# Query and key halves split on 128 partitions with their copies made by DMA, and the last gate job's S5 rows loaded whole

## The chip, the cores and the metric

The kernel runs on one core of a Trainium2 chip. The metric is the device time of one execution in microseconds; the time before is the median of three runs, 1220.09 us (1220.04 to 1220.55). The core's engines are named as in the profile: PE (TensorE, matmuls), PEld (its weight loads), DVE (VectorE), ACT (ScalarE), POOL (GpSimd) and SP (SyncE), whose queue issues nearly all DMAs.

## The reference

Two layers (`DEPTH = 2`) of a block on 1024 positions of width 1024, then a last RMS norm, all in float32. Of each layer:

```python
h = rms_norm(x, norm_w[l])
proj = h @ w_in[l]
fq, fk, fv, flog, su, rq, rk, rv, gate = split_cols(proj)
logf = log_sigmoid(flog + fox_b_f[l])
y_fox = forgetting_attention(fq, fk, fv, logf)      # 8 heads of 64, causal, softmax with decay
y_s5  = s5_layer(su, ...)                           # 16 groups of a complex scan, GLU
y_ret = retention(rotary(rq), rotary(rk), rv, ...)  # 4 heads of 64, group norm
y = concatenate([y_fox, y_s5, y_ret]) * silu(gate)
x = x + y @ w_out[l]
```

The scores of the attention are `q @ k / 8 + c_query - c_key`, with c the running sum of logf, masked to the past.

## The kernel before, in words

**Precision by halves.** A matmul on float32 takes longer than one on the rounded type `float32r`. So a large operand is split into a high part (a cast to float32r) and a low part (what the cast left over), and a product is the sum of three: high x high, high x low, low x high. `XH` and `XL` hold the normed input (later the gated output) in this form; `split_w` (line 306) does it for weights, in rings of two places each: `wr` raw, `wh` high, `wl` low.

**Projections.** A "job" (line 360) is 128 columns of the input projection. `granules` (line 320) runs the jobs one after another. A job has two parts of 512 positions (four of 256 for the last gate job), and a part is 24 matmuls into one of two PSUM banks (`ps_proj`), after which the job's `ev` reads the bank out. The next job's weights are loaded and split while the current one runs.

**Attention.** The 8 heads go in 4 pairs p. Each pair has four jobs, in this order: v, g (the gate), q, k. Here is what the change touches, in `fox_jobs` (line 458). The scores of one head are two matmuls with 128 rows each: `M` holds the head's 64 query rows, high and low one above the other, `T` holds the key's high rows twice, and `KL` the key's low rows of both heads:

- head A: `MA` = query high on partitions 0 to 63, low on 64 to 127; `TA` = key high on both halves;
- head B: `MB` and `TB` the other way about; `KL` = low of A over low of B.

So the query's `ev` (lines 465 to 470) makes two casts on ACT and two subtractions on DVE on 64 partitions each, and the key's `ev` (lines 475 to 482) two casts on ACT, two subtractions and two copies of the high rows to the other half on DVE. In `fox_rows` (line 518) POOL makes `zq` (M with the low half set to zero), PE multiplies `M` with `T` and `zq` with `KL` into `ps_s`, DVE adds the decay and takes the row minimum (`P`, `mn`), ACT the exponential, DVE the scaling. `turn` (line 566) has PE transpose P into `ps_t`, splits it into `pth` (ACT) and `ptl` (DVE), and PE multiplies these with the values into `ps_o`. The jobs of pair p+1 run among the attention of pair p; those after them need the attention of p done (`free`, line 509).

**Rings.** `slot(tag, ...)` takes a place of a ring in SBUF; a tile waits until the one before it in its place has been read for the last time. `th` has 2 places (used by v, g, the gate jobs and the output projection), `pt` has 5 (also for `pth`, `ptl`, `yt`), `wl` 2.

**Gate jobs.** `gate_job(l, x)` (line 1088) gates S5 rows (x = 0, 1) and retention rows (x = 2, 3): it loads the rows `y_d[4 + x]` to `yg`, multiplies, and splits the result. Jobs 0 and 1 are the last of a layer. Job 1 writes into XH and XL directly, in four parts of 256, while `y_loads` (line 1141) brings the other six blocks of rows, 768 KB for each DMA, over the parts of XH and XL that job 1 has finished with. Then `out_first` begins.

**What sets the order.** PE's order is written by hand through a planner (`Weave`, line 32): generators yield what they need, and the one that can run soonest by the planner's own costs (lines 109 to 147) goes next. For a DMA it charges

```python
if eng == "D":
    start += 1.0
    dur = max(out.nbytes(), 16384) / 360e3
...
end = start + dur + (2.0 if eng == "D" else 0.0)
```

one after another on one queue. The planner knows the PSUM banks, not the SBUF rings. The other engines' instructions and the DMAs are put in order by the framework's scheduler, from dependences, ring places and its own estimate; every engine, SP too, then works through its list in that order. Since engine calls go through the planner's recorder, every operation has line 158 in the profile; they are told apart by tile.

Of the kernel before, what the change touches and what calls it, by code (L numbers as in the profile page):

```python
# [9 lines left out]
F32 = mybir.dt.float32  # L10
F32R = mybir.dt.float32r
I32 = mybir.dt.int32
AF = mybir.ActivationFunctionType
ALU = mybir.AluOpType
AX = mybir.AxisListType

L = 1024
# [147 lines left out]
def need(*tiles, ps=(), ev=()):  # L165
    return tiles, ps, ev
# [3 lines left out]
def hybrid_block(ctx: ExitStack, tc: tile.TileContext, a: dict, out: bass.AP, taps=None):  # L170
# [5 lines left out]
    V, S, G, PE = (Clocked(W, k, e) for k, e in (("V", nc.vector), ("S", nc.scalar), ("G", nc.gpsimd), ("P", nc.tensor)))  # L176
    dma = Clocked(W, "D", nc.sync).dma_start
# [12 lines left out]
    def nm(s):  # L190
        uid[0] += 1
        return f"{s}_{uid[0]}"

    def slot(tag, shape, dt=F32, name=None):
        return sp.tile(shape, dt, tag=tag, name=nm(name or tag), bufs=NB[tag])

    def psum(tag, shape=(128, 512)):
        t = pp.tile(list(shape), F32, tag=tag, name=nm("ps_" + tag), bufs=PSUM[tag])
        W.psum(tag, t)
        return t  # L200
# [4 lines left out]
    def fr(ap):  # L205
        return ap.bitcast(F32)
# [44 lines left out]
    for c in (slice(0, 512), slice(512, 1024)):  # L251
        ps = psum("proj")
# [12 lines left out]
    y_d = dr.tile([KB, 128, L], F32, name="y_d")  # L265
# [94 lines left out]
    def job(l, col, start, perm=False, before=(), after=(), tags=("wh", "wl"), parts=2):  # L360
        src = a["w_in"][l, :, col:col + 128].rearrange("(k p) c -> p k c", p=128)
        return (lambda: split_w(src, 128, perm, tags)), start, before, after, parts

    def silu2(g2):

        def ev(n, sl, ps):
            th = slot("th", [128, 512], F32, "th")
            S.activation(out=th, in_=ps, func=AF.Tanh, scale=0.5)
            V.scalar_tensor_tensor(out=g2[:, sl], in0=th, scalar=1.0, in1=ps, op0=ALU.add, op1=ALU.mult)
        return ev  # L370
# [86 lines left out]

    def fox_jobs(l, p, tiles):
        qt = "qb" if p % 2 else "qa"

        def start_q():
            tiles.update((n, slot(qt, [128, L], F32R, n)) for n in ("MA", "MB", "TA", "TB", "KL"))
            MA, MB = tiles["MA"], tiles["MB"]

            def ev(n, sl, ps):
                S.copy(out=MA[0:64, sl], in_=ps[0:64])
                S.copy(out=MB[64:128, sl], in_=ps[64:128])
                V.tensor_tensor(out=MA[64:128, sl], in0=ps[0:64], in1=fr(MA[0:64, sl]), op=ALU.subtract)
                V.tensor_tensor(out=MB[0:64, sl], in0=ps[64:128], in1=fr(MB[64:128, sl]), op=ALU.subtract)
            return ev  # L470

        def start_k():
            TA, TB, KL = (tiles[n] for n in ("TA", "TB", "KL"))

            def ev(n, sl, ps):
                S.copy(out=TA[0:64, sl], in_=ps[0:64])
                S.copy(out=TB[64:128, sl], in_=ps[64:128])
                V.tensor_tensor(out=KL[0:64, sl], in0=ps[0:64], in1=fr(TA[0:64, sl]), op=ALU.subtract)
                V.tensor_tensor(out=KL[64:128, sl], in0=ps[64:128], in1=fr(TB[64:128, sl]), op=ALU.subtract)
                V.tensor_copy(out=TA[64:128, sl], in_=fr(TA[0:64, sl]))  # L480
                V.tensor_copy(out=TB[0:64, sl], in_=fr(TB[64:128, sl]))
            return ev

        def start_v():
            tiles.update((n, slot("v", [128, NT, 128], F32R, n)) for n in ("VA", "VB"))

            def ev(n, sl, ps):
                vt = slot("th", [128, 512], F32, "vt")
                S.copy(out=vt, in_=ps)
                W.add(values(n, vt), 2, SLACK["val"])  # L490
            return ev

        def values(n, vt):
            yield need(vt, ps=("t",))
            pt = psum("t", (128, 4, 128))
            for b in range(4):
                PE.transpose(pt[:, b, :], vt[:, b * 128:(b + 1) * 128], ident)
            for j, vx in enumerate((tiles["VA"], tiles["VB"])):
                src = pt[:, :, j * 64:(j + 1) * 64]
                hi = vx[:, 4 * n:4 * n + 4, 0:64]  # L500
                S.copy(out=hi, in_=src)
                V.tensor_tensor(out=vx[:, 4 * n:4 * n + 4, 64:128], in0=src, in1=fr(hi), op=ALU.subtract)
            W.done.add(("v", l, p, n))

        def start_g():
            tiles["g2"] = slot("gy", [128, L], F32, "g2")
            return silu2(tiles["g2"])

        free = {0: (("ret", l),), 1: (("ret", l), ("s5", l))}.get(p, (("att", l, p - 2),))
        return [job(l, C_V + p * 128, start_v, before={0: (), 1: (("mix", l),)}.get(p, free)),  # L510
                job(l, C_G + p * 128, start_g, before=() if p == 0 else free),
                job(l, C_Q + p * 128, start_q, before=free if p else (("mix", l),)),
                job(l, C_K + p * 128, start_k, after=(("k", l, p),))]
# [574 lines left out]
    def gate_job(l, x):  # L1088

        def start():  # L1090
            if x == 1:
                W.add(y_loads(l), 4)

            def ev(n, sl, ps):
                m = ps.shape[-1]
                y = slot("pt", [128, m], F32, "yg")
                dma(out=y, in_=y_d[4 + x, :, sl])
                th = slot("th", [128, m], F32, "th")
                S.activation(out=th, in_=ps, func=AF.Tanh, scale=0.5)
                V.scalar_tensor_tensor(out=th, in0=th, scalar=1.0, in1=ps, op0=ALU.add, op1=ALU.mult)  # L1100
                V.scalar_tensor_tensor(out=y, in0=y, scalar=0.125 if x < 2 else 0.5, in1=th, op0=ALU.mult, op1=ALU.mult)
                k = XPOS[4 + x]
                if x == 1:
                    S.copy(out=XH[:, k, sl], in_=y)
                    V.tensor_tensor(out=XL[:, k, sl], in0=y, in1=fr(XH[:, k, sl]), op=ALU.subtract)
                    W.mark(f"y5{l}.{n}")
                else:
                    yh, yl = th.bitcast(F32R), y.bitcast(F32R)
                    S.copy(out=yh, in_=y)
                    V.tensor_tensor(out=yl, in0=y, in1=th, op=ALU.subtract)  # L1110
                    dma(out=ys_d[k, :, 0, sl], in_=fr(yh))
                    dma(out=ys_d[k, :, 1, sl], in_=y)
            return ev

        return job(l, C_G + (4 + x) * 128, start, perm=x < 2, before=(("s5" if x < 2 else "ret", l),), after=(("gate", l, x),),
                   parts=4 if x == 1 else 2)
# [24 lines left out]
    def y_loads(l):  # L1141

        for n in range(4):
            yield need(ev=(("att", l, 2), ("gate", l, 1, n)))
            sl = slice(n * 256, (n + 1) * 256)
            for i, x in enumerate((XH, XL)):
                dma(out=fr(x[:, 0:6, sl]), in_=ys_d[:, :, i, sl].rearrange("k p c -> p k c"))
                W.mark(f"y{l}.{n}.{i}")
            W.done.add(("y", l, n))
# [68 lines left out]
    def trunk():  # L1218
# [10 lines left out]
        for l in range(depth):  # L1229
# [9 lines left out]
            for p in range(4):  # L1239
                tiles = {}  # L1240
                js = fox_jobs(l, p, tiles)

                def start_k(start=js[3][1], p=p, tiles=tiles):
                    W.add(fox_attend(l, p, tiles), 3)
                    return start()

                jobs += js[:3] + [(js[3][0], start_k, *js[3][2:])]
# [65 lines left out]
```

## Time and profile before

| | |
|---|---|
| median of three runs | 1220.09 us |
| the profiled execution | 1219.19 us, its span 1217.5 us |
| PE | 1163.4 us busy, 96% |
| DVE | 918.2 us, 75% |
| ACT | 559.1 us, 46% |
| POOL | 210.3 us, 17% |
| DMA | 140.64 MB, 37% of 16 engines on SP's queue |
| granted clock of PE | 0.98 of 2.4 GHz in the mean |

"Span" is the time from the first to the last instruction; the execution is 1.7 us longer. PE's busy time is modelled, since matmuls are pipelined: the end of one overlaps the next. In timelines, a bracket `[idle <-releaser]` says how long the engine stood idle ahead of a row and what ended that.

### The profile page before, as it was taken

Reading aid. Unit: us, or ns where it says so; the run is one execution under the profiler, and the core shown is the slowest. Engines: PE = TensorE matmul, PEld = TensorE weight load, DVE = VectorE, ACT = ScalarE, POOL = GpSimd, SP = SyncE. Lnnn points to the kernel's source line nnn. Section 1 sums busy time; section 2 is a strip of 40 time slices with the busy share of each in tenths; the row PEclk is TensorE's granted clock in tenths of the full one; section 3 lists DMA queues with packets and bytes.
Section 4 is the critical chain, followed back from the end, with each engine's and each line's share of the span. In section 5 each row is a group of like instructions: output and inputs, shape, how many; then the busy total and the mean of one; then the engine's idle time right before and its main releaser. Section 6 shows DMA issues by size and latency. Waiting matters only on the chain.

```text
span 1217.5 us, 18685 instructions
## 1 busy us (share of the span) xinstructions
PE 1163.4 (96%) x6320; PEld 989.2 (81%) x6320; DVE 918.2 (75%) x2611; ACT 559.1 (46%) x1085; POOL 210.3 (17%) x451
## 2 busy tenths in 40 slices
PE   8999989999799899999999999999999999989997
PEld 7878867878688787878889878778888888788886
DVE  7789696478778678786877856967877868968736
ACT  6526233445455455553243364335545545645411
POOL 0016222021122121210000163211212112112000
PEclk9999988999899999999999999999999999999999
DMA  7255324431112112838341845222233121274534
GB/s 231 58 158 176 115 71 132 140 125 52 61 35 71 53 43 78 271 115 231 101 153 59 258 112 146 63 92 73 61 109 109 57 57 53 82 233 154 170 107 156
DMA packets 137538, 140.64 MB, mean 116 GB/s; under 512 B 18849, under 2 KB 108641, under 8 KB 137442
## 3 DMA queue, kind: packets, MB, share of 16 engines
q1 hardware_dynamic: 137440, 139.44, 37.0%
q8 instruction: 50, 0.82, 0.3%
q14 instruction: 46, 0.38, 0.1%
q10 hardware_dynamic: 2, 0.00, 0.0%
HBM read 99.13 MB, written 40.29 MB: 115 GB/s over the span
## 4 chain that ended last, share of the span: by engine, by line
PE 50%; DVE 10%; issue 3%; ACT 2%; DMA 2%; POOL 0%; SPq 0%; DVEq 0%; ACTq 0%; POOLq 0%
PE ps_proj L158 37%; PE ps_s L158 5%; PE ps_o L158 4%; PE ps_t L158 4%; DVE P L158 2%; DMA yg<-y_d 1%; DVE ptl L158 1%; DVE wl L158 1%; DVE s5z L158 1%; DVE x L158 1%; DMA wor<-in_w_out_dram 0%; DVE g L158 0%; DVE KL L158 0%; DVE s5b L158 0%; ACT wh L158 0%
## 5 line engine op out<-in xcount | busy, mean ns | idle before, releaser
L158 PE MATMUL ps_proj<-XH,wh 128*128 128x512 f32 (+1 forms) x864 | 229.4, 395 | 3.9 <-DVE MB L158 2.6
L158 PE MATMUL ps_proj<-XH,wl 128*128 128x512 f32 (+1 forms) x864 | 228.3, 392 | 0.0
L158 PE MATMUL ps_proj<-XL,wh 128*128 128x512 f32 (+1 forms) x864 | 225.6, 388 | 0.0
L158 PEld LDWEIGHTS ps_proj<-XH,wh 128*128 128x128 f32 x864 | 159.1, 193 | 34.9 <-issue 3.0
L158 PEld LDWEIGHTS ps_proj<-XH,wl 128*128 128x128 f32 x864 | 157.8, 191 | 30.5 <-issue 0.5
L158 PEld LDWEIGHTS ps_proj<-XL,wh 128*128 128x128 f32 x864 | 157.0, 189 | 29.9 <-issue 0.5
L158 PE MATMUL ps_proj<-wo,XH 128*128 128x512 f32 x512 | 162.7, 394 | 0.0
L158 ACT ACTIVATE P<-P,mn 128x256 f32<-128x256 f32 (+7 forms) x128 | 99.5, 777 | 85.2 <-DVE mn L158 83.4
L158 DVE TENSOR_TENSOR ptl<-ps_t,pth 128x512 fp32r<-128x512 f32 (+1 forms) x160 | 99.2, 632 | 33.0 <-ACT pth L158 31.8
L158 ACT CAST pth<-ps_t 128x512 fp32r<-128x512 f32 (+1 forms) x160 | 85.0, 542 | 67.0 <-PE ps_t L158 52.3
L158 PEld LDWEIGHTS ps_proj<-wo,XH 128*128 128x128 f32 x512 | 95.3, 188 | 18.7
L158 DVE CUSTOM_DVE_ANT_0 P<-ps_s,negc,mn 128x128 f32<-128x128 f32 (+3 forms) x176 | 97.3, 553 | 7.3 <-PE ps_t L158 0.5
L158 PE MATMUL ps_proj<-wo,XL 128*128 128x512 f32 x256 | 100.5, 393 | 0.0
L158 DVE TENSOR_TENSOR wl<-wr,wh 128x1024 fp32r<-128x1024 f32 (+1 forms) x56 | 75.4, 1348 | 29.6 <-ACT wh L158 11.8
L158 PE MATMUL ps_t<-ident,P 128*128 128x128 f32 x576 | 87.0, 278 | 2.6 <-DVE P L158 2.5
L158 ACT CAST wh<-wr 128x1024 fp32r<-128x1024 f32 (+1 forms) x56 | 66.3, 1188 | 43.7 <-PE ps_proj L158 38.0
L158 PEld LDWEIGHTS ps_t<-ident,P 128*128 128x128 f32 x576 | 69.5, 144 | 8.8 <-issue 2.2
L158 POOL TENSOR_SCALAR_AFFINE_SELECT md<-negc 128x128 f32<-128x128 f32 x128 | 49.1, 384 | 149.4 <-DVE mn L158 72.1
L158 DVE TENSOR_SCALAR P<-P,rd 128x256 f32<-128x256 f32 (+7 forms) x128 | 66.8, 523 | 2.0
L158 POOL TENSOR_TENSOR rot<-rot,c_cos 128x512 f32<-128x512 f32 x16 | 27.4, 1711 | 232.7 <-ACT rot L158 231.6
L158 PE MATMUL ps_s<-KL,zq 128*128 128x256 f32 (+1 forms) x192 | 65.8, 343 | 0.0
L158 PE MATMUL ps_o<-ptl,VA 128*128 128x256 f32 x160 | 46.0, 310 | 16.3 <-DVE ptl L158 16.2
(259 smaller groups left out, 2033.0 us busy)
## 6 DMA issues: line engine op xcount, KB each, us to landing
wr<-in_w_in_dram SPq DMA_DIRECT2D x56, 512.0 KB, 4.1
negc<-negc_d SPq DMA_DIRECT2D x16, 512.0 KB, 3.7
wor<-in_w_out_dram SPq DMA_DIRECT2D x32, 256.0 KB, 3.4
ys_d<-yt SPq DMA_DIRECT2D x24, 256.0 KB, 2.4
XL<-ys_d SPq DMA_DIRECT2D x8, 768.0 KB, 10.0
XH<-ys_d SPq DMA_DIRECT2D x8, 768.0 KB, 7.0
xt<-x_d SPq DMA_DIRECT2D x24, 256.0 KB, 3.3
x_d<-xh SPq DMA_DIRECT2D x16, 256.0 KB, 3.5
```

Source lines behind the costliest of these rows:

```text
L158: r = f(*args, **kw)
```

## The change

In `fox_jobs`, the query's and the key's bank are cast and subtracted whole, on 128 partitions, into places of the ring `th`, and DMAs of 64 partitions by 512 columns bring the halves to their rows: four for a query part (two of the high half, two of the low half), four for a key part (each high half to both halves of its T). `KL` is written by the subtraction directly. In the last gate job (x = 1) the four loads of `yg` are replaced by two loads of half a row block each, into a place of the ring `wl`, asked for in the job's `start`, ahead of `y_loads`. The other gate jobs are as before.

```diff
 def start_q():
     def ev(n, sl, ps):
-        S.copy(out=MA[0:64, sl], in_=ps[0:64])
-        S.copy(out=MB[64:128, sl], in_=ps[64:128])
-        V.tensor_tensor(out=MA[64:128, sl], in0=ps[0:64], in1=fr(MA[0:64, sl]), op=ALU.subtract)
-        V.tensor_tensor(out=MB[0:64, sl], in0=ps[64:128], in1=fr(MB[64:128, sl]), op=ALU.subtract)
+        qh, ql = (slot("th", [128, 512], F32R, x) for x in ("qh", "ql"))
+        S.copy(out=qh, in_=ps)
+        V.tensor_tensor(out=ql, in0=ps, in1=fr(qh), op=ALU.subtract)
+        for M, r in ((MA, lo), (MB, up)):
+            dma(out=fr(M[r, sl]), in_=fr(qh[r]))
+        for M, r, o in ((MA, lo, up), (MB, up, lo)):
+            dma(out=fr(M[o, sl]), in_=fr(ql[r]))
 def start_k():
     def ev(n, sl, ps):
-        S.copy(out=TA[0:64, sl], in_=ps[0:64])
-        S.copy(out=TB[64:128, sl], in_=ps[64:128])
-        V.tensor_tensor(out=KL[0:64, sl], in0=ps[0:64], in1=fr(TA[0:64, sl]), op=ALU.subtract)
-        V.tensor_tensor(out=KL[64:128, sl], in0=ps[64:128], in1=fr(TB[64:128, sl]), op=ALU.subtract)
-        V.tensor_copy(out=TA[64:128, sl], in_=fr(TA[0:64, sl]))
-        V.tensor_copy(out=TB[0:64, sl], in_=fr(TB[64:128, sl]))
+        kh = slot("th", [128, 512], F32R, "kh")
+        S.copy(out=kh, in_=ps)
+        V.tensor_tensor(out=KL[:, sl], in0=ps, in1=fr(kh), op=ALU.subtract)
+        for r in (lo, up):
+            dma(out=fr(TA[r, sl]), in_=fr(kh[lo]))
+            dma(out=fr(TB[r, sl]), in_=fr(kh[up]))
 def gate_job(l, x):
     def start():
         if x == 1:
+            row = slot("wl", [128, L], F32, "yrow")
+            for c in (slice(0, 512), slice(512, L)):
+                dma(out=row[:, c], in_=y_d[5, :, c])
             W.add(y_loads(l), 4)
         def ev(n, sl, ps):
-            y = slot("pt", [128, m], F32, "yg")
-            dma(out=y, in_=y_d[4 + x, :, sl])
+            if x == 1:
+                y = row[:, sl]
+            else:
+                y = slot("pt", [128, m], F32, "yg")
+                dma(out=y, in_=y_d[4 + x, :, sl])
```

Here `lo` is partitions 0 to 63 and `up` 64 to 127.

## Rows read from the trace of the kernel before

**Rows 1.** The page's busy times: engine, us busy (share of the span), instructions.
```profile
PE 1163.4 (96%) x6320; PEld 989.2 (81%) x6320; DVE 918.2 (75%) x2611; ACT 559.1 (46%) x1085; POOL 210.3 (17%) x451
```
**Rows 2.** Waits of PE: engine, tile, what ended them, us in total, times, longest.
```profile
PE ps_o L158 <- DVE ptl L158: 18.2, 14, 4.0
...
PE ps_proj L158 <- DVE MB L158: 2.6, 1, 2.6
```
**Rows 3.** DVE's groups by shape: count, us busy, mean ns, idle before.
```profile
L158 DVE TENSOR_TENSOR ptl<-ps_t,pth 128x512 fp32r<-128x512 f32 x96 | 65.2, 685 | 19.8 <-ACT pth L158 18.9
...
L158 DVE TENSOR_TENSOR KL<-ps_proj,TB 64x512 fp32r<-64x512 f32 x16 | 11.1, 695 | 0.2
...
L158 DVE TENSOR_TENSOR KL<-ps_proj,TA 64x512 fp32r<-64x512 f32 x16 | 10.9, 681 | 1.9 <-ACT TB L158 1.5
...
L158 DVE CAST TA<-TA 64x512 fp32r<-64x512 f32 x16 | 6.9, 430 | 4.6 <-ACT TA L158 4.2
```
**Rows 4.** ACT's groups by shape: a copy on 128 partitions and a cast on 64.
```profile
L158 ACT COPY vt<-ps_proj 128x512 f32<-128x512 f32 x16 | 9.3, 584 | 15.8 <-PE ps_proj L158 15.0 <-ACT pth L158 0.7
...
L158 ACT CAST MA<-ps_proj 64x512 fp32r<-64x512 f32 x16 | 9.3, 578 | 7.3 <-PE ps_proj L158 7.2
```
**Rows 5.** PE's timeline: start us, us, operation, count [idle before <-releaser].
```profile
209.49 3.62 PE L158 MATMUL ps_proj<-XH,wh 128*128 128x512 f32 x8 [2.63 <-DVE MB L158]
212.95 2.00 PE L158 MATMUL ps_proj<-XL,wh 128*128 128x512 f32 x8
...
316.71 0.47 PE L158 MATMUL ps_s<-TB,MB 128*128 128x512 f32 x1 [2.05 <-DVE mn L158]
...
397.20 0.39 PE L158 MATMUL ps_o<-ptl,VA 128*128 128x256 f32 x1 [1.31 <-DVE ptl L158]
...
405.18 0.39 PE L158 MATMUL ps_o<-ptl,VB 128*128 128x256 f32 x1 [2.79 <-DVE x L158]
...
474.66 0.39 PE L158 MATMUL ps_o<-ptl,VA 128*128 128x256 f32 x1 [1.90 <-DVE ptl L158]
...
519.88 0.49 PE L158 MATMUL ps_o<-ptl,VA 128*128 128x256 f32 x1 [3.93 <-DVE ptl L158]
...
828.42 0.28 PE L158 MATMUL ps_s<-TA,MA 128*128 128x256 f32 x1
...
1059.45 0.58 PE L158 MATMUL ps_o<-ptl,VA 128*128 128x256 f32 x1 [2.23 <-DVE ptl L158]
...
1093.12 0.39 PE L158 MATMUL ps_o<-ptl,VA 128*128 128x256 f32 x1 [3.97 <-DVE ptl L158]
```
**Rows 6.** DVE's timeline ahead of those waits.
```profile
206.69 0.69 DVE L158 TENSOR_TENSOR MA<-ps_proj,MA 64x512 fp32r<-64x512 f32 x1
...
208.66 0.69 DVE L158 TENSOR_TENSOR MB<-ps_proj,MB 64x512 fp32r<-64x512 f32 x1
...
403.66 0.42 DVE L158 CAST TB<-TB 64x512 fp32r<-64x512 f32 x1
...
404.72 0.41 DVE L158 TENSOR_TENSOR x<-ps_o,x 64x256 f32<-64x256 f32 x1
...
514.78 0.43 DVE L158 SCALAR_TENSOR_TENSOR yg<-yg,th 128x256 f32<-128x256 f32 x1 [1.63 <-DMA yg<-y_d]
...
1087.36 0.43 DVE L158 SCALAR_TENSOR_TENSOR yg<-yg,th 128x256 f32<-128x256 f32 x1 [0.76 <-DMA yg<-y_d]
...
1091.23 0.43 DVE L158 SCALAR_TENSOR_TENSOR yg<-yg,th 128x256 f32<-128x256 f32 x1 [1.48 <-DMA yg<-y_d]
```
**Rows 7.** DMA issues: transfer, count, KB each, median us to landing.
```profile
wr<-in_w_in_dram SPq DMA_DIRECT2D x56, 512.0 KB, 4.1
...
ys_d<-th SPq DMA_DIRECT2D x12, 256.0 KB, 2.0
```
**Rows 8.** Waits of SP's queue: us in total, times, longest.
```profile
SPq L158 <- DVE yt L158: 115.0, 16, 14.3
```
**Rows 9.** ACT's timeline: the second layer's last key cast of its first pair.
```profile
824.67 0.58 ACT L158 CAST TA<-ps_proj 64x512 fp32r<-64x512 f32 x1 [0.81 <-PE ps_proj L158]
```

More of the change, by code (lines that the diff above doesn't have):

```diff
@@ L459, in fox_jobs @@
         qt = "qb" if p % 2 else "qa"
+        lo, up = slice(0, 64), slice(64, 128)
         def start_q():
```

## The prediction

> **What bounds the kernel now.** I read the page's busy shares first. TensorE is busy for 1163.4 of 1217.5 us [rows 1], so all that any edit can win is the idle 54.1 us, and what the lower clock costs after an idle stretch. Next the waits of PE: the largest entry by far is ps_o waiting for ptl, 18.2 us in 14 waits, all on VectorE (DVE), and one wait of ps_proj for MB [rows 2]. Then PE's timeline, for every row that carries an idle time in brackets: the eight that matter here are in [rows 5], 20.81 us together (2.63 + 2.05 + 1.31 + 2.79 + 1.90 + 3.93 + 2.23 + 3.97). DVE's timeline ahead of each shows two kinds. Six of them (the first five and the one at 1059.45) have the work of a query or key eviction queued on DVE ahead of what PE waits for; in [rows 6] the TB cast at 403.66 stands ahead of the x at 404.72 that ends the wait at 405.18, and KL, KL and TA stand ahead of that cast. The same pattern stands ahead of the waits at 316.71, 397.20, 474.66 and 1059.45. The other two (519.88 and 1093.12) have DVE itself waiting for the DMA of yg [rows 6], with the attention's ptl behind it.
>
> So DVE with its 75% is no bound over the whole span, but it is what ends PE's idle time at these eight places. In the second layer, apart from its last pair, hardly any idle time of PE is left to win: work taken off DVE there is worth nothing.
>
> **What the clock does.** After the wait of 2.63 us, eight 512-column matmuls take 3.62 us, and the eight after them 2.00 [rows 5]: a lower clock costs 1.62 us on top of the idle time. The 256-column matmuls at 1059.45 and 519.88 start with 0.58 and 0.49 us, against 0.39 at 405.18 [rows 5], so not every wait brings it: the one of 2.79 us did not.
>
> **The query eviction, 16 parts.** Before: two casts of 64 partitions on ACT and two subtractions on DVE. After: one of each on 128 partitions. A 128x512 subtraction from PSUM takes DVE 685 ns, a 64x512 one 685 to 695 [rows 3], and a 128x512 copy takes ACT 584 ns against 578 [rows 4]. So a part saves 0.69 us of DVE and 0.58 us of ACT: 11 and 9 us in all. On the path this counts at the first wait: the bank is now free after the MA row (206.69 + 0.69 = 207.38) instead of after MB (208.66 + 0.69 = 209.35), between which DVE does something else [rows 6]. Gain 1.97 us of the 2.63.
>
> **The key eviction, 16 parts.** Before: two subtractions and two casts on DVE, 681 + 695 + 430 + 430 ns; after, one subtraction of 685. A part saves 0.69 + 0.86 = 1.55 us of DVE [rows 3]; all 16 save 24.8 us, and ACT 9 us. On the path, by place: all 1.55 us ahead of the waits at 316.71, 405.18 and 1059.45; one KL and one TA cast, 0.69 + 0.43 = 1.12 us, ahead of those at 397.20 and 474.66, where the second cast follows the ptl. Each is smaller than its wait, so it is taken whole: 3 x 1.55 + 2 x 1.12 = 6.89 us. What is late next is the same ptl or P chain, with 0.2 to 1.2 us of the wait left.
>
> **The gate job's row.** Before, four yg loads of 256 columns, issued in turn among the large y loads; DVE stood idle for yg for 1.63 us in the first layer and 0.76 + 1.48 us in the second ahead of the matmul that PE waits for [rows 6]. After, the whole row is asked for once, as soon as gate job 0 has read its low parts for the last time, ahead of the y loads, and it has a whole part of gate job 1 (matmuls, tanh, one DVE operation) to arrive. I count DVE's idle time only, 1.63 + 2.24 = 3.87 us, since DVE then worked without a pause up to the ptl; the ends are 0 (the row queued behind the same loads) and PE's whole waits, 3.93 + 3.97 = 7.9 us. DVE's time is the nearer row, as the ptl can't pass it. The four ring places of pt that come free are costed at nothing: no wait in [rows 5] is for pt.
>
> **The clock's part.** Three of the waits fall below 0.9 us (209.49, 474.66, 1059.45). I count two clock losses of 1.62 us as gone, 3.2 us; the ends are 0 and six losses, 9.7 us.
>
> **What is added: 128 DMAs of 128 KB**, four for each part, all on SP's queue. An issue takes about 0.33 us of SP, 1.3 us a part; SP has room, and each weight load behind it is asked for a whole job ahead. The trace has no move from SBUF to SBUF. The nearest rows are the stores of th, 256 KB in 2.0 us, and the weight loads, 512 KB in 4.1 us [rows 7]; I take 2.2 us, near the store. So T is ready 0.58 + 1.3 + 2.2 = 4.1 us after the cast starts (6.0 with the load's time). The first score that reads it comes 3.75 us after the last key cast in the second layer's first pair (824.67 to 828.42) [rows 5, 9], about as long in its third, and 9 us or more in the other six. PE's order is written by a planner that charges the moves 1.0 + 4 x 0.36 + 2.0 us and puts projection matmuls there instead; I charge 1 us at each of the two, ends 0 and 2.3.
>
> **The ring th has two places.** A query part holds both until its moves have been read. Its low half leaves at cast 0.58 + subtraction 0.69 + issue 0.7 + 2.2 = 4.2 us at the earliest; the next part's cast comes three times 2.00 us later at the earliest [rows 5], mostly later, as the attention is woven in. I charge 0.9 us in all. Without that cover each of 16 second parts holds ACT, and with it the pth casts that the attention waits for.
>
> The Trainium skill, "SBUF — State Buffer", section "Door 1: The DMA port swizzle", says that 64 partitions reach only half of the DMA ports, and a later section that two transfers to the two halves run one after the other; estimated from its 196 GB/s, a move would take 2 + 0.67 us and the four of a part would queue, some 2 us more in all. No row here shows such a move. By it the hold would be about 6.2 us, over the shortest distance of two parts, and the charge for th some 2 us more, and it adds weight to the slower rival below.
>
> **Sum.** 1.97 + 6.89 + 3.87 + 3.2 = 15.9 us gained; 2.0 + 0.9 = 2.9 us lost; net 13.0. The profiled execution took 1219.19 us (span 1217.5, 1.7 around it): 1206.2. The median of the runs shown is 0.9 us above it, so about **1207**. The planner's new order of PE moves every place above by some microseconds; I cost that at 0, between 4 us either way.
>
> **The rivals.**
> - *Only the gate's row pays* (1213 to 1217). The planner charges T to come later than before, spreads the attention anew, and DVE's savings fall where PE has other work, as in most of the second layer. For it: 16 parts of each kind and only six waits behind them. What is left is 3.87 us, one clock loss and 1 or 2 of the waits, less the costs: 1220.1 - 5 = 1215.
> - *The moves stand behind a parked SP* (slower, 1222 to 1235). SP works in order and stood up to 14.3 us waiting for a yt, 115 us over 16 times [rows 8]. If a move sits behind such a wait, the place in th is not given back, the next cast holds ACT, and PE runs out of banks. It decides once the hold passes the distance of two parts, 6 us. At 2.5 us for half of the 32 parts, 40 us are lost on ACT; if half of that reaches PE, 20 against 15.9 gained: 1224. Against it: 115 us are 9% of the span, so most moves meet a free SP, and a part that follows in the attention comes later than the shortest distance.
> - *No change* (1218 to 1222): stalls shift to ptl behind ACT's pth, as the wait chain of the attention also runs through ACT; gain and costs 3 us each.
> - *All of it pays* (1190 to 1200): the eight waits, 20.81 us, and six clock losses, 9.7 us, are 30 us at most and give 1190; most of both gives 1196.
> - That the change does not do what it says I exclude for DVE's count; that the row arrives no earlier is inside the first rival's range.
>
> **How the numbers follow.** Forecast (1201 to 1213) 0.52, only the gate's row 0.18, parked SP 0.15, no change 0.07, all of it 0.08. What this kernel's measurement tells from no change is about 0.2%, 2.4 us. Faster takes the forecast, the all-of-it case and the gate's row: 0.78. Within 0.2%: 0.07. Slower: 0.15. The range that leaves out 2 in 10 is 1196 to 1223: the lower part of "all of it" and most of the parked case lie outside. The forecast's own range is 1201 to 1213.
>
> **What would show it.** DVE's busy time falls by 36 us, ACT's by 18; q1 carries some 16.8 MB more. PE's waits for ptl fall from 18 us towards 8; no DVE row waits for yg. Wrong if ACT shows waits for DMAs into MA, MB, TA or TB of more than 5 us in all, if PE waits for those DMAs, or if PE's idle time stays near 54 us while DVE's busy time has fallen: then DVE was in front of PE, but not what ended the waits.

## The result, and the profile after

The changed kernel takes **1203.55 us** (median of 4 runs, 1201.77 to 1207.68), the kernel before 1220.07 beside it: ratio 0.9867, 95% interval [0.9843, 0.9891], a gain of 16.5 us where 13.0 were forecast. Run again later it took 1202.10 us, ratio 0.9854 [0.9838, 0.9870]. The trace below is of the slowest of the first four runs (1207.68 us, span 1206.0); a second trace, of a run of 1200.67 us (span 1198.9), is used beside it, and every engine's instructions stand in the same order there.

Busy times of after, to be held against [rows 1], and the first line of the queues (packets, MB, share of 16 engines' span):
```profile
PE 1159.5 (96%) x6320; PEld 986.2 (82%) x6320; DVE 882.6 (73%) x2547; ACT 539.7 (45%) x1053; POOL 207.5 (17%) x451
...
q1 hardware_dynamic: 147104, 156.22, 43.9%
```
DVE fell by 35.6 us and ACT by 19.4 (36 and 18 were expected). The span fell by 11.5 us in this execution: 3.9 us of PE's busy time for the same matmuls, and 7.6 us of its idle time (54.1 to 46.5). In the second trace PE is busy for 1154.7 us, at a mean granted clock of 0.987 and not 0.983, so two executions of one kernel differ by 4.8 us in this.

Waits of PE after, which answer to [rows 2] (what ended them, us in total, times, longest):
```profile
PE ps_o L158 <- DVE ptl L158: 7.7, 8, 2.0
...
PE ps_proj L158 <- DVE ql L158: 2.6, 1, 2.6
...
PE ps_t L158 <- DVE P L158: 2.4, 1, 2.4
PE ps_t L158 <- ACT vt L158: 2.0, 1, 2.0
```
The ptl waits went from 18.2 to 7.7 us. Two waits that were to shrink or not to be there stand beside them: the one for the query's bank, now ended by ql, and a new one for vt. PE's timeline has them, and what is left of [rows 5]:
```profile
210.14 3.53 PE L158 MATMUL ps_proj<-XH,wh 128*128 128x512 f32 x8 [2.61 <-DVE ql L158]
...
232.24 0.66 PE L158 MATMUL ps_t<-ident,vt 128*128 128x128 f32 x4 [2.02 <-ACT vt L158]
...
318.93 0.39 PE L158 MATMUL ps_o<-ptl,VA 128*128 128x256 f32 x1 [1.75 <-DVE ptl L158]
...
398.96 0.38 PE L158 MATMUL ps_o<-ptl,VB 128*128 128x256 f32 x1 [1.54 <-DVE x L158]
...
475.48 0.39 PE L158 MATMUL ps_o<-ptl,VB 128*128 128x256 f32 x1 [0.23 <-DVE x L158]
...
1081.24 1.76 PE L158 MATMUL ps_t<-ident,P 128*128 128x128 f32 x7 [2.42 <-DVE P L158]
```
In the second trace PE waits 2.41 us at 210.82 as well, and 2.42 us for P at 1080.10, but not for vt (231.17). The first layer's gate stage, 3.93 us of waiting at 519.88 before, has no wait at all. No DVE row waits for yrow's DMA; a yg of another gate job still waits for 0.87 us, at 487.33.

Where the wait at 210 comes from is read on two engines. POOL and DVE of after, ahead of it:
```profile
201.60 0.29 POOL L158 TENSOR_SCALAR_AFFINE_SELECT zq<-MA 128x128 fp32r<-128x128 f32 x1 [10.90 <-DMA MA<-ql]
...
202.67 2.55 POOL L158 TENSOR_TENSOR s5bs<-s5bs,s5Ei 128x512 f32<-128x512 f32 x2
```
```profile
204.00 1.76 DVE L158 TENSOR_TENSOR s5b<-s5b,s5bs 128x512 f32<-128x512 f32 x1 [2.91 <-POOL s5bs L158]
...
209.43 0.66 DVE L158 TENSOR_TENSOR ql<-ps_proj,qh 128x512 fp32r<-128x512 f32 x1
```
Four zq selections, which read M whole, stand in POOL's order ahead of the s5bs product. They wait for the DMA of M's low rows; s5bs waits behind them, DVE waits 2.91 us for s5bs, and ql stands behind the S5 scans at 209.43. Before, the two subtractions stood at 206.69 and 208.66 [rows 6].

### The profile page after: what moved, and what is told of

Read it like the earlier page. It is cut to its first block, busy times and chain, and to the rows that moved or that the text cites. A ratio compares the mean times of both kernels' runs of the same rounds, so it can differ in the third digit from the quotient of the medians.

```text
span 1206.0 us, 18908 instructions
## 1 busy us (share of the span) xinstructions
PE 1159.5 (96%) x6320; PEld 986.2 (82%) x6320; DVE 882.6 (73%) x2547; ACT 539.7 (45%) x1053; POOL 207.5 (17%) x451
## 3 DMA queue, kind: packets, MB, share of 16 engines
q1 hardware_dynamic: 147104, 156.22, 43.9%
## 4 chain that ended last, share of the span: by engine, by line
PE 46%; DVE 6%; DMA 2%; ACT 1%; issue 1%; POOL 0%; DVEq 0%; ACTq 0%; SPq 0%
PE ps_proj L158 34%; PE ps_s L158 5%; PE ps_o L158 4%; PE ps_t L158 3%; DMA wor<-in_w_out_dram 1%; DMA XH<-ys_d 1%; DVE P L158 1%; DVE s5z L158 1%; DVE s5b L158 0%; DVE ptl L158 0%; DVE x L158 0%; DVE wl L158 0%; ACT s5bs L158 0%; DVE s5pw L158 0%; DVE wo L158 0%
## 5 line engine op out<-in xcount | busy, mean ns | idle before, releaser
L158 PE MATMUL ps_proj<-XH,wl 128*128 128x512 f32 (+1 forms) x864 | 225.8, 389 | 0.0
L158 PE MATMUL ps_proj<-wo,XH 128*128 128x512 f32 x512 | 165.7, 399 | 0.0
L158 ACT ACTIVATE xs<-xt 128x1024 f32<-128x1024 f32 (+1 forms) x26 | 25.9, 996 | 77.4 <-DVE xt L158 74.4
```

The source lines that it names most:

```text
L158: r = f(*args, **kw)
```

## The experiments

PE's order is written by the planner from the costs it charges, so every edit rewrites it. Two sorts of kernel are used: some in which the planner charges what the kernel issues ("replanned" in the table), and some in which it is charged for the other kernel's instructions, so that PE's 6320 matmuls stand in exactly the order of before (or of after), and waits can be compared matmul by matmul. That holds PE's order alone: those of ACT, DVE, POOL and SP are made anew for every kernel. Kernels of the second sort show the recording line 158 as 187.

| kernel | median us | ratio to before [95%] |
|---|---|---|
| old instructions, new order | 1220.11 | 0.9996 [0.9986, 1.0005] |
| new instructions, old order | 1204.28 | 0.9872 [0.9857, 0.9887] |
| row alone, old order | 1210.49 | 0.9918 [0.9901, 0.9934] |
| key alone, old order | 1214.17 | 0.9953 [0.9937, 0.9970] |
| row alone, replanned | 1214.15 | 0.9943 [0.9924, 0.9963] |
| key alone, replanned | 1216.67 | 0.9972 [0.9960, 0.9985] |
| query alone, replanned | 1216.10 | 0.9960 [0.9945, 0.9975] |
| query and key, replanned | 1207.27 | 0.9892 [0.9874, 0.9911] |
| after, late zq | 1202.82 | 0.9867 [0.9845, 0.9889] |
| late zq, first pair's key as before | 1200.75 | 0.9832 [0.9813, 0.9851] |
| new instructions, old order, moves twice | 1197.59 | 0.9814 [0.9796, 0.9833] |

### The instructions or the order of PE's work

The instructions are issued past the planner, and what the other kernel would issue is charged to it. For the key, with the new instructions in the old order:
```diff
+nc.scalar.copy(out=kh, in_=ps)
+nc.vector.tensor_tensor(out=KL[:, sl], in0=ps, in1=fr(kh), op=ALU.subtract)
+for r in (lo, up):
+    nc.sync.dma_start(out=fr(TA[r, sl]), in_=fr(kh[lo]))
+    nc.sync.dma_start(out=fr(TB[r, sl]), in_=fr(kh[up]))
+W.as_if("S", TA, [ps])
+W.as_if("S", TB, [ps])
+W.as_if("V", KL, [ps, TA])
+W.as_if("V", KL, [ps, TB])
+W.as_if("V", TA, [TA], True)
+W.as_if("V", TB, [TB], True)
```


> The instructions of after (128-partition casts and subtractions, moves by DMA, whole row), but the planner is charged for those of before, so that TensorE's instructions stand in exactly the order of before. Theory: the waits at 316, 397, 405, 475, 520, 1059 and 1093 us shrink as forecast, as each is ended by DVE's queue: 1203 to 1209 us. Rival (the gain needs the new order, in which projections stand where the moves land): 1215 to 1222 us.

> The instructions of before (casts, subtractions, four yg loads), but the planner is charged for those of after, so that TensorE's instructions stand in exactly the order of after. Theory (taking work off DVE is what pays, the order alone is worth nothing): 1217 to 1226 us, with the waits for ptl back near 18 us. Rival (the new order of TensorE's work brings the gain): 1203 to 1209 us.

The new instructions in the old order took 1204.28 us, the old ones in the new order 1220.11. So PE's order alone is worth nothing (under 1.7 us either way), and the new instructions bring the gain without it; the rival "the planner's order does it" falls. How much of the gain comes from the orders that ACT, DVE and POOL were given around the new instructions isn't shown. PE's timeline of the new instructions in the old order, at the same matmuls as [rows 5] (209.49, then one that had no wait, 316.71, 405.18, 474.66, 519.88, 1093.12):
```profile
210.33 3.54 PE L187 MATMUL ps_proj<-XH,wh 128*128 128x512 f32 x8 [2.61 <-DVE ql L499]
...
232.18 0.66 PE L187 MATMUL ps_t<-ident,vt 128*128 128x128 f32 x4 [3.20 <-ACT vt L187]
...
318.93 0.47 PE L187 MATMUL ps_s<-TB,MB 128*128 128x512 f32 x1 [0.18 <-DVE mn L187]
...
404.90 0.39 PE L187 MATMUL ps_o<-ptl,VB 128*128 128x256 f32 x1 [1.07 <-DVE x L187]
...
473.16 0.39 PE L187 MATMUL ps_o<-ptl,VA 128*128 128x256 f32 x1 [0.72 <-DVE ptl L187]
...
512.92 0.36 PE L187 MATMUL ps_o<-ptl,VA 128*128 128x256 f32 x1 [0.77 <-DVE ptl L187]
...
1078.94 0.39 PE L187 MATMUL ps_o<-ptl,VA 128*128 128x256 f32 x1
```
Read as start against start: 0.8 us behind at 210, 4.1 behind at 232 (228.09 before), 2.2 behind at 319, then 0.3 ahead, 1.5, 7.0, and 14.2 ahead at 1078.94. Seven of the eight waits are shorter or gone (those at 397.20 and 1059.45 are 0.00), and together they are 5.4 us, where they were 20.81; the first is not shorter, and the one at 232 is a loss of 3.2 us. The old instructions in the new order wait 11.6 us for ptl and 5.8 us for x, 17.4 together. The kernel before waits 18.2 and 2.8 us under these two names, 21.0, so the 18 us expected for ptl did not come back whole, though the time did.

### Which part is worth what

Each part alone in the old order, with the edit above for that part and the rest of the kernel as before.

> Only the gate job's row is loaded whole; TensorE's instructions stand in the order of before. By the first forecast (DVE's idle time for yg counts): 3.87 us and at most a clock loss, 1214.5 to 1216.5 us. Rival (TensorE's whole waits of 3.93 and 3.97 us go, with one clock loss): 1210 to 1213 us.

> Only the key eviction is that of after; TensorE's instructions stand in the order of before. Theory (1.55 us of DVE per key part ends five waits; eight moves near 215 to 222 us cost a late vt, 3.3 us in the mixed kernel): 6.9 us and one or two clock losses gained, 2 to 4 lost: 1212 to 1216 us, with TensorE waiting for vt near 232 us. Rival (half of what the mixed kernel won in the first layer's attention came from the query's subtractions): 1216 to 1219 us.

Row 9.7 us, key 6.0, together 15.7, and all three parts in that order 15.7. The key came out as its theory said, the row as its rival did. If parts add, the query's part is worth about nothing there (the intervals leave some 3 us either way); the query alone was not run in this order, and in the replanned kernels below the parts do not add. The five waits that the key's term was to shrink, in the trace of key alone:
```profile
320.03 0.47 PE L187 MATMUL ps_s<-TB,MB 128*128 128x512 f32 x1 [0.19 <-DVE mn L187]
...
400.48 0.39 PE L187 MATMUL ps_o<-ptl,VA 128*128 128x256 f32 x1 [0.57 <-DVE ptl L187]
...
406.73 0.38 PE L187 MATMUL ps_o<-ptl,VB 128*128 128x256 f32 x1 [1.08 <-DVE x L187]
...
476.09 0.39 PE L187 MATMUL ps_o<-ptl,VA 128*128 128x256 f32 x1 [1.75 <-DVE ptl L187]
...
1058.25 0.39 PE L187 MATMUL ps_o<-ptl,VA 128*128 128x256 f32 x1
```
They fell from 10.28 us to about 3.7.

The row is worth nearly PE's whole waits and the clock behind one of them, not DVE's idle time. The wait of 3.93 us is 0.77 in its trace and that of 3.97 is gone, 7.1 us less; behind the second, 1.6 us more are gained within 4 us (1093.12 against 1084.22, then 1096.87 against 1086.35), where the granted clock was 0.53 to 0.61 of 2.4 GHz before (1093 to 1097) and is 1.00 now. Why is read on PE, DVE and ACT in the second layer's gate stage, of row alone in the old order:
```profile
1081.76 0.49 PE L187 MATMUL ps_t<-ident,P 128*128 128x128 f32 x3
...
1081.83 0.42 DVE L187 TENSOR_TENSOR XL<-yrow,XH 128x256 fp32r<-128x256 f32 x1
...
1082.72 0.47 ACT L187 CAST pth<-ps_t 128x384 fp32r<-128x384 f32 x1
...
1083.05 0.41 DVE L187 SCALAR_TENSOR_TENSOR th<-th,ps_proj 128x256 f32<-128x256 f32 x1
1083.38 0.55 DVE L187 TENSOR_TENSOR ptl<-ps_t,pth 128x384 fp32r<-128x384 f32 x1
1083.85 0.47 DVE L187 SCALAR_TENSOR_TENSOR yrow<-yrow,th 128x256 f32<-128x256 f32 x1
```
and of the kernel before at the same place, around the row of 1091.23 in [rows 6]:
```profile
1086.54 0.49 PE L158 MATMUL ps_t<-ident,P 128*128 128x128 f32 x3
...
1091.69 0.40 ACT L158 CAST XH<-yg 128x256 fp32r<-128x256 f32 x1 [1.14 <-DVE yg L158]
1092.00 0.47 ACT L158 CAST pth<-ps_t 128x384 fp32r<-128x384 f32 x1
...
1091.77 0.42 DVE L158 TENSOR_SCALAR P<-P,rd 128x384 f32<-128x384 f32 x1
1092.13 0.43 DVE L158 TENSOR_TENSOR XL<-yg,XH 128x256 fp32r<-128x256 f32 x1
1092.51 0.56 DVE L158 TENSOR_TENSOR ptl<-ps_t,pth 128x384 fp32r<-128x384 f32 x1
```
The ptl subtracts the pth from what PE transposed. From the end of the transposes to the end of the ptl 6.0 us pass before (1087.03 to 1093.07), 1.7 us with the row at hand (1082.25 to 1083.93). Before, the gate's second part got its product at 1091.23, when its yg had landed, and two engines were held by it: on ACT the pth stood behind that part's cast, which waited 1.14 us for the product, and on DVE the scaling of P and the part's XL subtraction stood ahead of the ptl. With the row at hand this part is done when the transposes end (1081.83 + 0.42 = 1082.25). The scaling of that P (128x384) is not among the rows ahead of the ptl either, as DVE's order changed too. PE's matmul, 3.97 us late before, follows at 1084.22 with no wait.

The same parts with the planner charging what is issued; of the row's edit, for the job x = 1:
```diff
-dma(out=y, in_=y_d[4 + x, :, sl])
+y = row[:, sl]
```


> Only the gate job's row is loaded whole; query and key evictions as before. Theory (DVE's idle time for yg set the two gate stages): the two waits of 3.93 and 3.97 us shrink by 3.87 us together and one clock loss of 1.6 us goes: 1213 to 1217 us. Rival (those waits only shift to the next ptl or P once the row is there): 1218 to 1221 us. Second rival (the row is worth PE's whole waits of 7.9 us and two clock losses): 1209 to 1212 us.

> Key eviction as after, query eviction and gate row as before. Theory (1.55 us of DVE per key part is what stood in front of five waits): 6.9 us and one or two clock losses less 1 to 2 us for a late T: 1210 to 1214 us; and POOL's zq doesn't wait for a DMA, so the attention of the first pair starts at about 255.6 us as before, not at 258.4. Rival (T's later arrival takes it back): 1218 to 1222 us.

> Query eviction as after, key eviction and gate row as before. Theory (the four zq on POOL wait for the moves of the low rows and hold the s5bs product, so the first pair starts 2.8 us later; the 11 us taken off DVE lie mostly beside the waits): 1217 to 1223 us, with zq waiting for a DMA ahead of s5bs near 200 us. Rival (the query's DVE time is worth its 1.97 us and a clock loss, as first forecast): 1214 to 1217 us.

> Query and key evictions as after, gate row as before (four yg loads). Theory (eight waits, six of them behind the evictions): the key's 6.9 us and one or two clock losses are won, less the late zq on POOL in the first layer, and the gate's 3.9 to 7.9 us are missing: 1207 to 1212 us. Rival 'only the gate's row pays': 1216 to 1221 us.

Row 6.3 us, key 3.8, query 4.3, query and key 13.2. The row came out as forecast in its time, but not in its mechanism: in its trace the two gate waits are down to 0.8 us together, and its own order of PE brings a new wait of 2.17 us for s5R (599.04). Query and key together came out as forecast; key alone missed its range by 2.7 us and lies between its two theories. Query alone fits the rival: its trace has the zq waiting 10.79 us for a DMA ahead of s5bs, as expected, but the first pair starts at 256.5 us, 0.8 late and not 2.8, and the last ptl of the first layer's attention is multiplied 4.2 us earlier than before (561.30 against 565.50). What one part is worth moves by 2 to 4 us with the order that the planner writes, and query and key together give 5 us more than alone: each alone leaves 20.1 (query) or 17.4 us (key) of waits for ptl, both together 5.1.

### The wait at 210 and the new one at 232

```diff
+with tc.issue_after(s5g[0].ins):
     G.affine_select(out=zq, in_=M[:, qs], pattern=[[0, 128]], compare_op=ALU.is_ge, fill=0.0,
```
(s5g[0] is the last s5zs product.)

> The kernel of after, with one edge more: on POOL the zq selections stand behind the last s5zs product, instead of ahead of s5bs in the first layer; all other engines keep their order. Theory (zq waits 10.9 us for the moves of the low rows and holds s5bs, the s5 chain and with it the first pair's start by 2.8 us): the waits at 210 and 232 us (2.61 + 2.02 us and a clock loss of 1.5 us) go and the first pair starts 2 to 3 us earlier: 3 to 6 us under the kernel of after. Rival (the start of the first pair is given back by later waits): within 1.5 us of it.

> The changed kernel once more, beside the three others on the same chip: 1201 to 1208 us by all theories, as the level against which the late zq and the two mixed kernels are read.

The reason for the wait at 210 is confirmed, the gain isn't: 1202.82 us against 1202.10. The four zq selections are all that stands elsewhere on any engine. PE with the late zq:
```profile
208.76 2.11 PE L158 MATMUL ps_proj<-XH,wh 128*128 128x512 f32 x8 [0.40 <-DVE ql L158]
...
230.35 0.66 PE L158 MATMUL ps_t<-ident,vt 128*128 128x128 f32 x4 [2.48 <-ACT vt L158]
```
The first wait is 0.40 us, and eight matmuls take 2.11 us instead of 3.53: the granted clock stays at 1.00 of 2.4 GHz from 209 to 213 us, where after has 0.50, the lower level of 1.2 GHz (211 to 213). In this execution most of what was won is waited for 22 us later, for vt. That wait changes from one execution to the next, for with the same orders the second trace of after has none (PE and ACT):
```profile
231.17 0.66 PE L158 MATMUL ps_t<-ident,vt 128*128 128x128 f32 x4
...
225.61 1.06 ACT L158 ACTIVATE s5q<-s5y 128x1024 f32<-128x1024 f32 x1 [5.01 <-DMA s5y<-yd_d]
```
So where the late zq's gain went is not settled by one trace. On ACT vt stands behind s5q, which waits for a load. ACT of the new instructions in the old order:
```profile
226.61 1.06 ACT L187 ACTIVATE s5q<-s5y 128x1024 f32<-128x1024 f32 x1 [6.69 <-DMA s5y<-yd_d]
230.11 1.06 ACT L187 ACTIVATE s5q<-s5q 128x1024 f32<-128x1024 f32 x1 [2.44 <-DVE s5q L187]
231.07 0.57 ACT L187 COPY s5Y<-ps_s 128x512 f32<-128x512 f32 x1
231.54 0.59 ACT L187 COPY vt<-ps_proj 128x512 f32<-128x512 f32 x1
```
Before, this s5q began at 219.04, 4.4 us after SP issued the load (214.68); here 8.3 us after (218.28). Ahead of it in SP's queue stand four moves of the key, behind it four more. From issue to use the load takes 4.4 to 6.1 us in the six traces without the first pair's key moves, and 6.7 to 10.3 us in the seven with them (the doubled moves below apart); the 6.7 is the second trace of after. The windows (busy times, granted clock, DMA share, GB/s) show the DMA engines then, first the kernel before:
```profile
217.00:219.00 2.00, 2.00 (x10) 1.63 (x9) 0.34 (x1) 0.35 (x1) 0.00 (x0) 1.00 0.82 235
219.00:221.00 2.00, 2.00 (x11) 1.60 (x10) 0.89 (x1) 1.95 (x3) 0.81 (x1) 1.00 0.50 180
```
then the new instructions in the old order, where the share stays over 1 from 216 to 228 us:
```profile
218.00:220.00 2.00, 2.00 (x10) 1.66 (x9) 0.61 (x1) 1.34 (x3) 0.00 (x0) 1.00 1.04 218
220.00:222.00 2.00, 2.00 (x10) 1.61 (x10) 1.22 (x2) 0.00 (x0) 0.00 (x0) 1.00 1.09 256
```
Two runs test this. In one the first pair's key is evicted as before, with no moves, beside the late zq; in the other each move is issued a second time, to memory:
```diff
 def move(out, in_):
     nc.sync.dma_start(out=out, in_=in_)
+    nc.sync.dma_start(out=twice_d[nth[0]], in_=in_)
```


> The kernel with the late zq, and in the first pair of each layer (4 of 16 key parts) the key evicted as before, by casts, with no moves; TensorE's order is that of after. Theory (eight key moves fill the DMA engines ahead of the load of s5y, which ends the wait for vt): s5y lands in 4 to 5 us after its issue, the wait of 2.5 us at 230 us goes and the 0.4 us at 209 us stay: 3 to 5 us under the kernel of after, 1197 to 1200 us. Rival (the start of the first pair is given back by later waits, as with the late zq alone): within 1.5 us of it, 1201 to 1204 us.

> The new instructions in the old order, and each of the 128 moves issued a second time, to memory (128 KB each, nothing reads it). Theory (a move costs only where the DMA engines are full, in the stretch of 216 to 228 us with the first pair's eight key moves): 1 MB more there, by 0.62 us of the 16 engines a move some 5 us more of a wait for vt; elsewhere nothing: 1206 to 1211 us. Rival (SP's issues, 0.5 us each, and the two places of th are the price): 64 us more of issues, a hold past the distance of two parts, waits of ACT for th: 1214 to 1235 us.

Without the first pair's key moves the vt wait is gone, but the old key eviction brings a wait of its own (1.79 us for KL at 225.56), and s5q still began 6.1 us after the issue (221.54 against 215.42). The 1200.75 us lie between the two theories; the intervals of this kernel and of after overlap.

The moves issued twice gave the surprise: **1197.59 us, 6.7 us less** than the same kernel with each move once. Both theories expected more time. Its PE has 0.29 us of wait at 207.15 and none for vt; by the vt matmul (224.61 against 232.18) it is 7.6 us ahead (0.9 of it from before 200 us, 2.3 from the shorter wait at 210, 1.2 from the clock behind that, 3.2 from the wait for vt), and of that 4.7 are left at the end. Its ACT:
```profile
222.03 0.59 ACT L187 COPY s5Y<-ps_s 128x512 f32<-128x512 f32 x1 [6.32 <-PE ps_s L187]
222.51 0.59 ACT L187 COPY vt<-ps_proj 128x512 f32<-128x512 f32 x1
...
231.97 1.06 ACT L187 ACTIVATE s5q<-s5y 128x1024 f32<-128x1024 f32 x1 [0.34 <-DMA s5y<-yd_d]
```
PE's order is the same. Those of ACT, POOL and DVE are made at the build from its own estimates, and with more moves in the program they came out otherwise: vt stands ahead of s5q, and the first s5bs product ahead of the zq selections. So the moves' transfers are not the price by themselves. The price is what stands behind an instruction that waits for a move (s5bs behind zq) or for a load which the moves made late (vt behind s5q). This kernel's interval lies below that of after (0.9838 to 0.9870). The same orders with each move once were not tried, so that these two places make the difference is argued from the timelines.

## Why the prediction was right, point by point

- **What bounds: right.** Taking work off DVE, and the wait for yg with it, shortened seven of the eight waits at the very matmuls named, from 20.81 to 5.4 us together with PE's order held; PE's order alone gave nothing, as costed.
- **Query, 1.97 us: wrong.** The step read "the bank is now free after the MA row". The subtraction did fall into one, but DVE came to it later: the zq selections on POOL read M whole, so the moves added a DMA to an instruction that stood ahead of s5bs. The prediction followed who waits for T and for th, and not who else reads M. With zq moved the wait fell to 0.40 us.
- **Key, 6.89 us: right in size.** Alone in the old order the five waits fell by 6.6 us. By place it is less even: the one at 474.66 fell by 0.15 and not 1.12, those at 316.71 and 1059.45 by more than forecast. Against it stand 2.38 us of a wait for vt (the matmul comes at 231.92 against 228.09) and longer waits elsewhere, 5.23 us at 520.33 where 3.93 were. That execution was the slowest of its eight; the median says 6.0 us net.
- **Gate row, 3.87 us: mis-sized.** The statement that failed is "I count DVE's idle time only". It took DVE's work between the yg product and the ptl as fixed, and did not look at ACT, where the pth stood behind a cast of the same part. All of that came late with yg, and with the row at hand it was done early or stood behind the ptl. The ptl did not pass the product, as was said, but its delay was longer than DVE's idle time. The term measures 9.7 us with PE's order held (7.1 of PE's waits and 1.6 of clock are read in the trace), 6.3 with it replanned, where a new wait took 2.2. The upper end that was given, 7.9, was the nearer one.
- **Clock, 3.2 us: not shown.** PE's busy time fell by 3.9 us in the one trace of after and by 8.7 in the other, by 5.0 with the new instructions in the old order (1158.4): two executions of one kernel differ by more than the term. By place, the loss behind 1093.12 is gone (1.6 us), the one at 209.49, which was counted as gone, is still there (3.53 us for eight matmuls).
- **Costs, 2.9 us: the place is wrong, the amount open.** PE never waits for a T, also at the second layer's first pair, where 1 us was charged; and ACT never waits for a move out of th in after. What was lost stands at 232 us, 2.0 us in one trace of after, nothing in the other and 3.2 in the old order: vt behind a load among the moves. Nine in ten issues of a move took 0.46 to 0.60 us of SP, not 0.33.
- **The rule that was weighed.** A move costs the DMA engines (43.9% of 1206.0 us less 37.0% of 1217.5) / 128 = 0.62 us of all 16. The Trainium skill, "SBUF — State Buffer", "Door 1: The DMA port swizzle", has 64 partitions reach half of the ports; the 0.67 us estimated from its 196 GB/s lie near that, though 0.62 is a share of the engines' time and not a move's duration. The 2 us more of hold that were estimated on top did not show as a wait on ACT.
- **Rivals.** "Only the gate's row pays" falls (query and key give 13.2 us without it). "Parked SP" falls: with 256 moves in place of 128 the kernel was not slower. Its picture was half right: a load, not th, stood behind the moves.
- **The second layer** gave its 3.97 us at 1093.12 partly back: in the new order a chain of P holds PE for 2.42 us at 1081.24, in old instructions and new alike. So does a wait for s5R, new in that order: 2.45 us at 589.33 (2.47 at 600.84 with the old instructions).
- **The sum** is in part luck. Its 13.0 us, against 16.5 measured, hold 1.97 us of the query that weren't there, and the row brought more than twice its term: two misses of opposite sign.

Open stays the query's own share, between nothing (old order, if the parts add) and 4.3 us (replanned), and with it what the remade orders of ACT, DVE and POOL are worth.

## What to carry to other kernels

When an engine's write becomes a DMA, list every reader of the tile, on all engines, and look at what stands behind each of them in its engine's order; the loss came through two queues that the edit didn't touch (POOL's zq, which reads the tile, and ACT's s5q, which waits for a load behind the moves). When a wait ends on a load, look at what hangs on it on every engine: here its price was nearer the consumer's whole wait than one engine's idle time. Hold the order of the bounding engine fixed to price the parts, and then try orders: here they moved the time by as much as a part of the edit did (6.7 us). And take a second trace before a single wait is given a cause.

## What the runs showed of the hardware

128 KB from 64 partitions of SBUF to 64 others landed in a median of 2.2 to 2.4 us, near the 2.0 us of the 256 KB stores [rows 7], as far as the trace of after knows their landing (19 of 128 moves); MA's low rows, 4.2 us, are one landing. Eight of them were issued within 8 us around 219 us, among weight loads and yg loads. The DMA share was over 1 for 12 us then (new instructions in the old order), a key's move took up to 7.3 us to land (after), and the s5y load went from 4.4 to 8.3 us between issue and use.
